# The last LayerNorm of a two-layer decoder: the mean taken from a column of weight sums, the squares of three quarters of the columns taken beside the last product, the square root on ScalarE

## Chip, cores and metric

The kernel runs on one core of one Trainium2 chip. The metric is device time in microseconds (us), as the median of several runs. Lower is better.

## The reference

What is computed is a decoder of two layers over 256 tokens of width 1024. Layer 0 mixes tokens with a gated spatial unit, layer 1 with causal attention; each is followed by a gated MLP with a short convolution. After each of the four sub-layers stands a residual sum and a LayerNorm. What matters here is the last one:

```python
def layer_norm(x, g, b):
    xf = x.astype(jnp.float32)
    mu = jnp.mean(xf, axis=-1, keepdims=True)
    var = jnp.mean(jnp.square(xf - mu), axis=-1, keepdims=True)
    y = (xf - mu) * lax.rsqrt(var + LN_EPS)
    return (y * g.astype(jnp.float32) + b.astype(jnp.float32)).astype(x.dtype)
...
    return (jax.nn.gelu(g) * val) @ w_down
...
        y = conv_ffn(x, f_w_up[i], f_conv_w[i], f_conv_b[i], f_w_down[i])
        x = layer_norm(DN_ALPHA * x + y, ln_ffn_g[i], ln_ffn_b[i])
```

`w_down` is 2816 x 1024. The result of the last `layer_norm` is the output, 256 x 1024 in float32.

## The kernel before, in words

All weights are streamed from memory in chunks of 128 x 2048 float32 into two buffers (`raw`). ScalarE rounds each half of a chunk to the matmul's reduced float32 format (`whi`), and VectorE takes the remainder (`wlo = raw - whi`); `prep` (L436) records both through `split` (L377). Five chunks are held at once, ten tiles of 1024 columns each in `whi` and in `wlo`. A product of full accuracy is then three matmuls: high by high, high by low, low by high (`rows_step`, L622).

Nothing is emitted in the order of the source. Each step is recorded as an operation with an engine, a price in ns and its dependences (`Plan.op`, L90). `Plan.emit` (L125) simulates the five engines with these prices: TensorE's main stream keeps the order of recording, and on the other engines the operation with the earliest due time among the ready ones goes next. The result is a fixed program for each engine; each engine works its list in order and waits on semaphores.

The output projections, the last of them (`f_dn1`) among them, go through `project_out` (L652). The 256 tokens are two row tiles, t = 0 and t = 1. The sum runs over 22 tiles of 128 weight rows (k). For k = 0 to 15 both row tiles are accumulated together in four PSUM banks of 512 columns. For the last six k (`TAIL`), t = 0 is finished first, then t = 1. For t = 1 the right bank is added into `x` early (`add(*mine.pop())`, L689), and the last six k of the right half go into two fresh half-banks of 256 columns (`ends`, L690). So the very end of TensorE's work is, in this order: 18 matmuls of 512 columns for columns 0 to 511, 18 of 256 columns for 512 to 767, and 18 of 256 columns for 768 to 1023 (`cuts[1]`, L661).

As each piece is done, `stats` (L556) adds it into `x` on VectorE (L360) and takes its partial mean and variance (`bn_stats`, L563); after the third piece it joins the three (`bn_aggr`, L566), adds epsilon (L568), and GpSimd raises the sum to the power -0.5 (L569). Then `scaled` (L573) works on VectorE: two steps of 512 columns, (x - mean) * gamma, which need no power, and then four of 256 columns, x * rstd + beta, which do. Behind each of these four a store to the output is issued from SyncE's queue (L374). The row of gamma and beta is the tile `lnrow`.

All of VectorE's steps of the form (a op s) op b are recorded on L360, plain sums, products and differences on L356, all of ScalarE's on L350, all main matmuls on L338, so that the tile names and shapes tell them apart. `tensor_tensor_reduce` (L952, in the softmax) shows in the trace as CUSTOM_DVE_ANT_0 with a short READ_ACCUMULATOR behind it.

Of the kernel before, what the change touches and what calls it, by code (L numbers as in the profile page):

```python
# [237 lines left out]
def trunk_kernel(ctx: ExitStack, tc: tile.TileContext, a: dict, out: bass.AP):  # L238
# [8 lines left out]
    def tiles(name, n, cols, dtype=F32):  # L247
        return [sb.tile([P, cols], dtype, name=f"{name}{i}") for i in range(n)]

    whi, wlo = Ring(tiles("whi", 2 * CHUNKS, SUB, F32R)), Ring(tiles("wlo", 2 * CHUNKS, SUB, F32R))  # L250
    raws = Ring(tiles("raw", RAWS, CH))

    xt = sb.tile([P, 2 * KT * S], F32R, name="xt")
# [11 lines left out]
    def place(which, at, cols):  # L265

        t = rr if which == "rr" else ff
        prev = [b for s, e, b in owners[which] if s < at + cols and at < e]
        b = Buf(t[:, at:at + cols], prev)
        owners[which] = [x for x in owners[which] if not (at <= x[0] and x[1] <= at + cols)] + [(at, at + cols, b)]  # L270
        return b
# [80 lines left out]
    def dve(ns, emit, r, w):  # L352
        return plan.op("dve", ns, emit, r, w)
# [23 lines left out]
    def split(hi, lo, src, psum=False, by="act"):  # L377

        (hb, hp, hv), (lb, lp, lv), (xb, xp, xv) = hi, lo, src
        if by == "dve":  # L380
            dve(70 + 0.52 * flat(xv), lambda: nc.vector.tensor_copy(hv, xv), [(xb, xp)], [(hb, hp)])  # L381
        else:
            act(hv, xv, AF.Copy, [(xb, xp)], [(hb, hp)], psum=psum)
        return tt(lv, xv, hv.bitcast(F32), ALU.subtract, [(xb, xp), (hb, hp)], [(lb, lp)])
# [49 lines left out]
        return [(raw, b, e, s * SUB) for s in range(2) for b, e in cuts]  # L434

    def prep(i):  # L436
        subs = []
        for raw, b, e, at in pieces_of(i):
            if b == 0:
                hi, lo = whi.new(), wlo.new()  # L440
                subs.append((hi, lo))
            parts = range(b // 256, e // 256)
            low = split((hi, parts, hi.ap[:, b:e]), (lo, parts, lo.ap[:, b:e]),
                        (raw, parts if 2 * i < KHEAD else range((at + b) // 256, (at + e) // 256),
                         raw.ap[:, at + b:at + e]), by="act" if loads.get("low") else "dve")
            loads.setdefault("low", low)
        chunks[i] = subs

    FINE = set()
    for n in ("f_up0", "f_up1"):  # L450
        FINE |= set(range(where[n, 0], where[n, 5]))

    def sub(name, c, s):
        return chunks[where[name, c]][s]
# [41 lines left out]
    def ln_rows(i):  # L496
        b = rowring.new()
        src = a["lnrow"]
        o = load(b.ap, bass.AP(tensor=src.tensor, offset=src.offset + i * 2 * D, ap=[[0, P], [1, 2 * D]]), [b])
        if i == 0:  # L500
            o.after = loads[5]
        return b, b.ap.rearrange("p (a d) -> p a d", a=2)
# [70 lines left out]
    def scaled(r, x, st, mean, rstd, rows, to=None):  # L573
# [6 lines left out]
        for o, n in [(o, S) for o in range(0, D, S)]:  # L580
# [3 lines left out]
            if to is not None:  # L584
                load(to[:, sl], x[:, sl], (), [(r, parts)])

    def ln_back(r, st, mean, rstd, rows, t, li, h, l, waits):

        step = KT // len(waits)
        lc = lncol.ap.rearrange("p (i a k) -> p i a k", i=3, a=2)  # L590
        x = r.ap
        for k0 in range(0, KT, step):
            sl, parts = slice(k0 * P, (k0 + step) * P), range(k0 // 2, (k0 + step) // 2)
            ts(x[:, sl], x[:, sl], mean, rstd, ALU.subtract, ALU.mult,
               [(r, parts), (st, ["mv", "rstd"])], [(r, parts)])

        def rest():
            rb, rv = rows
            for op, j in ((ALU.mult, 0), (ALU.add, 1)):
                for o in (0, HALF):  # L600
                    sl, parts = slice(o, o + HALF), range(o // S, (o + HALF) // S)
                    tt(x[:, sl], x[:, sl], rv[:, j, sl], op, [(r, parts), rb], [(r, parts)])

        def turn(k0):
            pt, x32 = bank(), (x32a if step == 4 else x32b).new()
            transposes([(pt.ap[:, j * P:(j + 1) * P], x[:, (k0 + j) * P:(k0 + j + 1) * P]) for j in range(step)],
                       [(r, range(k0 // 2, (k0 + step) // 2))], [pt])
            for j in range(step):
                k = k0 + j
                act(x32.ap[:, j * P:(j + 1) * P], pt.ap[:, j * P:(j + 1) * P], AF.Identity, [pt, lncol], [(x32, [j])],  # L610
                    bias=lc[:, li, 1, k:k + 1], scale=lc[:, li, 0, k:k + 1], psum=True)
            parts = [(t, k) for k in range(k0, k0 + step)]
            split((h, parts, xt_view(h)[:, t, k0:k0 + step, :]), (l, parts, xt_view(l)[:, t, k0:k0 + step, :]),
                  (x32, range(step), x32.ap.rearrange("p (k c) -> p k c", k=step)))
            if k0 + step == KT:
                plan.later(REST[li], rest)

        for wait, k0 in zip(waits, range(0, KT, step)):
            plan.later(wait, lambda k0=k0: turn(k0))


    def rows_step(pieces, hk, lk, r, hi, lo, first, last, into=None):  # L622


        groups = []
        for i, (o, n, b) in enumerate(pieces):
            parts = range(o // 256, (o + n) // 256)
            seq = [(b.ap[:, :n], x, w.ap[:, o:o + n], first and j == 0, last and j == 2)
                   for j, (x, w) in enumerate([(hk, hi), (hk, lo), (lk, hi)])]
            if into is not None:  # L630
                into += [(i, (0, 2, 1)[j], q) for j, q in enumerate(seq)]
            groups.append(mms(seq, r + [(hi, parts), (lo, parts)], [b], into=into,
                              ready=into is not None and len(into) == 12))
        plan.tick()
        return groups
# [16 lines left out]
    def project_out(name, nk, at, xold, li, rows_i):  # L652

        last = li is None

        rows = None if name == "b_o" else ln_rows(rows_i)


        free = [bank(True) for _ in range(2 * NT)]
        pieces = [[(o, HALF, free[2 * t + o // HALF]) for o in (0, HALF)] for t in range(NT)]  # L660
        cuts = [[(0, HALF), (HALF, HALF)], [(0, HALF), (HALF, S), (HALF + S, S)]]  # L661
        ends = []

        def step(t, k, which, first=0, last=nk - 1):
            hi, lo = sub(name, k // 2, k % 2)
            hk, lk, r = at(k, t)
            return rows_step(which, hk, lk, r, hi, lo, k == first, k == last)

        start = nk - TAIL
        early = [(k, t) for k in range(start) for t in range(NT)]  # L670
        for k, t in sorted(early, key=lambda x: x[1]) if nk == KT else early:
            step(t, k, pieces[t][:1])
            groups = step(t, k, pieces[t][1:], last=nk - 1 if t == 0 else start - 1)
            if name == "f_dn0" and (k, t) == (3, NT - 1):
                state["table"].after = groups[-1]
            if k % 2 and t == NT - 1:
                spent(name, k // 2)
        res = (None, None) if last else xt_new()
        for t in range(NT):
            r, x = xold[t], xold[t].ap  # L680

            def add(o, n, b, by=ALPHA):
                parts = range(o // S, (o + n) // S)
                stt(x[:, o:o + n], x[:, o:o + n], by, b.ap[:, :n], ALU.mult, ALU.add, [(r, parts), b], [(r, parts)])
                done_with(b)

            mine = list(pieces[t])
            if t == NT - 1:
                add(*mine.pop())  # L689
                ends = [(o, n, half()) for o, n in cuts[t][1:]]  # L690
                mine += ends
            both = start, nk - 2 if t == 0 and nk == KT else start
            turns = [(p, k) for k in range(*both) for p in mine] + [(p, k) for p in mine for k in range(both[1], nk)]
            for p, k in turns:
                if t == 0 and k == nk - 2:
                    plan.tick(AHEAD)
                step(t, k, [p], first=start if p in ends else 0)
            if t == NT - 1:
                for k in range(start, nk, 2):
                    spent(name, k // 2)  # L700

            rows = rows or ln_rows(rows_i)
            st, mean, rstd = stats(r, x, cuts[t], lambda j, o, n: add(*mine[j], 1.0 if mine[j] in ends else ALPHA))
            if last:
                scaled(r, x, st, mean, rstd, rows, out[t * P:(t + 1) * P, :])
            else:
                ln_back(r, st, mean, rstd, rows, t, li, *res, T0_WAITS if t == 0 else T1_WAITS)
        return res
# [428 lines left out]
```

## Time and profile before

| | |
|---|---|
| median of 3 runs | 563.37 us (563.23 to 564.23) |
| profiled execution, its own time | 563.43 us |
| profiled execution, span from first to last instruction | 561.7 us |
| granted TensorE clock, mean | 0.996 |
| busy: TensorE / VectorE / ScalarE / GpSimd | 98% / 83% / 64% / 2% |

The time of an execution is its span and 1.7 us around it. In the lists of groups, the first time is the group's busy total in us and the second the mean of one instruction in ns; in timelines and in the chain of waits the first number is the start in us from the span's start, the second the length in us. Several rows of one kind that follow each other are merged, with their count behind an x, and the brackets tell how long the engine sat idle ahead of a row and what ended that. PE is TensorE, DVE is VectorE, ACT is ScalarE, POOL is GpSimd, SPq is SyncE's queue of transfers.

### The profile page before, as it was taken

Reading aid. Unit: us, or ns where it says so; the run is one execution under the profiler, and the core shown is the slowest. Engines: PE = TensorE matmul, PEld = TensorE weight load, DVE = VectorE, ACT = ScalarE, POOL = GpSimd, SP = SyncE. Lnnn points to the kernel's source line nnn. Section 1 sums busy time; section 2 is a strip of 40 time slices with the busy share of each in tenths; the row PEclk is TensorE's granted clock in tenths of the full one; section 3 lists DMA queues with packets and bytes.
Section 4 is the critical chain, followed back from the end, with each engine's and each line's share of the span. In section 5 each row is a group of like instructions: output and inputs, shape, how many; then the busy total and the mean of one; then the engine's idle time right before and its main releaser. Section 6 shows DMA issues by size and latency. Waiting matters only on the chain.

```text
span 561.7 us, 8289 instructions
## 1 busy us (share of the span) xinstructions
PE 552.4 (98%) x3042; PEld 473.7 (84%) x3042; DVE 467.8 (83%) x902; ACT 361.3 (64%) x679; POOL 11.2 (2%) x18
## 2 busy tenths in 40 slices
PE   9999999999999999999999999999999999999994
PEld 6888788988988888888888888788888988888884
DVE  5798989999899989558868778899999999998326
ACT  6647577777777667425677867587777787685200
POOL 0020000000000000001000000000000000000001
PEclk9999999999999999999999999999999999999998
DMA  8987445756645366852657252725667454557202
GB/s 320 371 307 280 160 149 175 276 175 219 235 196 183 117 242 219 301 192 79 232 207 220 87 182 82 293 88 195 245 228 285 162 221 156 200 202 272 75 1 75
DMA packets 19569, 110.97 MB, mean 198 GB/s; under 512 B 2295, under 2 KB 5577, under 8 KB 7369
## 3 DMA queue, kind: packets, MB, share of 16 engines
q1 hardware_dynamic: 19528, 110.44, 54.8%
q8 instruction: 24, 0.39, 0.3%
q14 instruction: 17, 0.13, 0.1%
HBM read 109.36 MB, written 1.07 MB: 197 GB/s over the span
## 4 chain that ended last, share of the span: by engine, by line
PE 92%; DMA 3%; DVE 3%; ACT 1%; issue 0%; DVEq 0%; ACTq 0%
PE bank L338 58%; PE twos L338 32%; DMA raw<-in_a_out 1%; PE twos L344 1%; DMA raw<-in_a_u 1%; PE bank L344 1%; DVE wlo L356 1%; DVE ff L356 1%; DMA ff<-in_head 1%; DVE x L360 0%; ACT whi L350 0%; DVE rr L356 0%; ACT rr L350 0%; DVE stat L563 0%; DVE whi L381 0%
## 5 line engine op out<-in xcount | busy, mean ns | idle before, releaser
L356 DVE TENSOR_TENSOR wlo<-raw,whi 128x1024 fp32r<-128x1024 f32 (+1 forms) x202 | 220.2, 1114 | 28.4 <-ACT whi L350 28.1
L350 ACT ACTIVATE whi<-raw 128x1024 fp32r<-128x1024 f32 (+1 forms) x202 | 187.5, 966 | 41.6 <-DMA raw<-in_f_dn 16.8
L338 PE MATMUL bank<-whi,rr 128*128 128x512 f32 x432 | 135.7, 391 | 0.5 <-DVE ff L356 0.5
L338 PE MATMUL bank<-xt,whi 128*128 128x512 f32 x512 | 121.2, 391 | 0.0
L338 PEld LDWEIGHTS bank<-xt,whi 128*128 128x128 f32 x512 | 94.7, 188 | 18.7
L338 PEld LDWEIGHTS bank<-whi,rr 128*128 128x128 f32 x432 | 81.1, 188 | 18.1 <-DVE ff L356 0.9
L338 PE MATMUL bank<-wlo,rr 128*128 128x512 f32 x216 | 84.1, 389 | 0.0
L338 PE MATMUL twos<-xt,whi 128*128 128x512 f32 x320 | 74.4, 390 | 0.0
L360 DVE SCALAR_TENSOR_TENSOR ff<-ff,convc 128x255 f32<-128x255 f32 (+1 forms) x160 | 69.5, 478 | 3.1 <-ACT ff L350 2.6
L338 PEld LDWEIGHTS twos<-xt,whi 128*128 128x128 f32 x320 | 59.4, 188 | 11.9
L338 PEld LDWEIGHTS bank<-xt,wlo 128*128 128x128 f32 x512 | 64.2, 191 | 2.0 <-issue 0.3
L338 PE MATMUL bank<-xt,wlo 128*128 128x256 f32 x512 | 65.6, 284 | 0.0
L350 ACT ACTIVATE ff<-ff,convc 128x256 f32<-128x256 f32 x80 | 45.1, 593 | 10.4 <-DVE ff L356 10.3
L338 PEld LDWEIGHTS bank<-wlo,rr 128*128 128x128 f32 x216 | 40.6, 188 | 8.1
L338 PE MATMUL twos<-whi,xt 128*128 128x512 f32 x128 | 42.1, 396 | 0.0
L350 ACT ACTIVATE ff<-ff 128x256 f32<-128x256 f32 x52 | 20.5, 412 | 31.8 <-DVE rr L356 26.0
L338 PEld LDWEIGHTS twos<-xt,wlo 128*128 128x128 f32 x320 | 39.7, 192 | 0.8
L338 PE MATMUL twos<-xt,wlo 128*128 128x256 f32 x320 | 40.0, 283 | 0.0
L350 ACT ACTIVATE ff<-bank 128x256 f32<-128x256 f32 (+2 forms) x62 | 24.2, 394 | 16.0 <-PE bank L338 14.7
L350 ACT ACTIVATE ff<-bank,lncol 128x128 f32<-128x128 f32 x48 | 18.9, 459 | 22.8 <-PE bank L344 18.8
L338 PEld LDWEIGHTS twos<-whi,xt 128*128 128x128 f32 x128 | 24.1, 188 | 4.7
L350 ACT ACTIVATE ff<-twos 128x512 f32<-128x512 f32 (+1 forms) x34 | 17.7, 551 | 15.7 <-PE twos L338 13.0
(88 smaller groups left out, 514.2 us busy)
## 6 DMA issues: line engine op xcount, KB each, us to landing
raw<-in_f_up SPq DMA_DIRECT2D x44, 1024.0 KB, 4.8
raw<-in_f_dn SPq DMA_DIRECT2D x22, 1024.0 KB, 4.8
raw<-in_b_qk SPq DMA_DIRECT2D x8, 1024.0 KB, 4.8
lnrow<-in_lnrow SPq DMA_DIRECT2D x5, 1024.0 KB, 8.4
raw<-in_a_out SPq DMA_DIRECT2D x4, 1024.0 KB, 7.0
raw<-in_b_v SPq DMA_DIRECT2D x4, 1024.0 KB, 4.8
raw<-in_b_o SPq DMA_DIRECT2D x4, 1024.0 KB, 4.8
raw<-in_a_u SPq DMA_DIRECT2D x3, 1024.0 KB, 9.4
```

The costliest lines, as they stand in the source:

```text
L338: nc.tensor.matmul(o, l, x, start=start, stop=stop)
L344: nc.tensor.transpose(o, x, ident.ap)
L350: return plan.op("act", ns, lambda: nc.scalar.activation(o, x, func, **kw), r, w, table=table)
L356: return dve(70 + 1.04 * flat(x), lambda: nc.vector.tensor_tensor(o, x, y, op=op), r, w)
L360: lambda: nc.vector.scalar_tensor_tensor(o, x, s, y, op0=op0, op1=op1), r, w)
```

## The change

Only the last normalization, and of it only t = 1, gets a new form; it needs a sum of weights that is made ahead.

- `whi` and `wlo` tiles get two more columns. For the three chunks of the last six k of `f_dn1` (`SUMMED`), VectorE sums the weights of columns 512 to 767 of each row, splits the sum into high and low part, and puts it into the two columns (twice the same).
- The last two pieces of t = 1 change places, and the last but one takes the sums along: 18 matmuls of 258 columns give columns 768 to 1023 and the row sum of the product that is still to come (columns 512 to 767).
- `close` replaces `stats` and `scaled` for t = 1. The early-added part of columns 512 to 767 is put through `bn_stats` at once, columns 0 to 511 when they are done; the piece of 256 columns is added by a `tensor_tensor_reduce` that also gives its sum and starts from the sum of the coming product. So the mean of all 1024 columns is known before the last product is.
- Under the last product: ScalarE takes the squares of 768 columns with an accumulated sum; VectorE subtracts the mean from columns 512 to 767 in place and makes (x - mean) * gamma for the other 768. Gamma has been scaled by the square root of 1024 on ScalarE beforehand, into a part of `ff`.
- Behind the last product: VectorE adds it; GpSimd multiplies these 256 columns by gamma; VectorE takes their squares' sum; ScalarE takes the square root of the total; VectorE inverts it and makes three steps y * rstd + beta, of 512, 256 and 256 columns, each with its store.

```diff
-    whi, wlo = Ring(tiles("whi", 2 * CHUNKS, SUB, F32R)), Ring(tiles("wlo", 2 * CHUNKS, SUB, F32R))
+    whi, wlo = (Ring(tiles(n, 2 * CHUNKS, SUB + 2, F32R)) for n in ("whi", "wlo"))
...
+            if i in SUMMED and e == SUB:
+                if sums is None:
+                    sums = stat.new()
+                    both_subs = raw.ap[:, :CH].rearrange("p (a c) -> p a c", a=2)[:, :, HALF:HALF + S]
+                    dve(70 + 1.04 * 2 * S, lambda: nc.vector.tensor_reduce(
+                        sums.ap[:, :2], both_subs, axis=mybir.AxisListType.X, op=ALU.add),
+                        [(raw, [2, 6])], [sums])
+                split((hi, [4], hi.ap[:, SUB:]), (lo, [4], lo.ap[:, SUB:]),
+                      (sums, [0], sums.ap[:, at // SUB:at // SUB + 1].to_broadcast([P, 2])), by="dve")
...
+    SUMMED = set(range(where["f_dn1", (FT - TAIL) // 2], where["f_dn1", FT // 2 - 1] + 1))
...
+    def close(r, x, own, rows, to):
...
+        act(gd.ap, rv[:, 0], AF.Copy, [rb], [gd], scale=D ** 0.5)
...
+        def summed(o, v, w, op, first, to, r, w_):
+            dve(70 + 1.04 * flat(v), lambda: nc.vector.tensor_tensor_reduce(
+                out=o, in0=v, in1=w, scale=1.0, scalar=first, op0=op, op1=ALU.add, accum_out=to), r, w_)
+
+        some(1, x2, p2)
+        act(junk.ap[:, :1], st.ap[:, 6:7], AF.Sqrt, [(st, [("st", 1)])], [junk], table="sqrt")
+        stt(x0, x0, ALPHA, b0.ap[:, :n0], ALU.mult, ALU.add, [(r, p0), b0], [(r, p0)])
+        some(0, x0, p0)
+        dve(90, lambda: nc.vector.bn_aggr(st.ap[:, 12:14], st.ap[:, :12]), [(st, [("st", 0), ("st", 1)])], [(st, ["mv"])])
+        dve(70, lambda: nc.vector.tensor_scalar_mul(known, mean, (n0 + n2) / D), [(st, ["mv"])], [(st, ["known"])])
+        summed(x1, x1, b1.ap[:, :n1], ALU.add, b1.ap[:, n1:n1 + 1], total, [(r, p1), b1], [(r, p1), (st, ["total"])])
+        dve(130, lambda: nc.vector.scalar_tensor_tensor(less, total, -1.0 / D, known, op0=ALU.mult, op1=ALU.subtract),
+            [(st, ["total", "known"])], [(st, ["less"])])
+        less_ = (st, ["less"])
+        for j, v, p, to_ in ((j0, x0, p0, ss0), (j1, x1, p1, ss1)):
+            act(j, v, AF.Square, [(r, p), less_], [(junk, [p[0]]), (st, [("ss", j is j1)])], bias=less, accum=to_)
+        act(rest, ss1, AF.Identity, [(st, [("ss", False), ("ss", True)])], [(st, ["rest"])], bias=ss0)
+        dve(190, lambda: nc.vector.tensor_scalar(x2, x2, less, None, op0=ALU.add), [(r, p2), less_], [(r, p2)])
+        for v, w, g, p in ((y0, x0, g0, p0), (y1, x1, g1, p1)):
+            stt(v, w, less, g, ALU.add, ALU.mult, [(r, p), less_, gd], [(y, p)])
+        tt(x2, x2, b2.ap[:, :n2], ALU.add, [(r, p2), b2], [(r, p2)])
+        plan.op("pool", 1060, lambda: nc.gpsimd.tensor_tensor(y2, x2, g2, op=ALU.mult), [(r, p2), gd], [(y, p2)])
+        summed(j2, x2, x2, ALU.mult, D * EPS, ssl, [(r, p2)], [(junk, [p2[0]]), (st, ["ssl"])])
+        act(rstd, ssl, AF.Sqrt, [(st, ["ssl", "rest"])], [(st, ["std"])], bias=rest, table="sqrt")
+        dve(80, lambda: nc.vector.reciprocal(rstd, rstd), [(st, ["std"])], [(st, ["rstd"])])
+        for o, v, p in ((o0, y0, p0), (o1, y1, p1), (o2, y2, p2)):
+            stt(v, v, rstd, rv[:, 1, o:o + flat(v)], ALU.mult, ALU.add, [(y, p), (st, ["rstd"]), rb], [(y, p)])
+            load(to[:, o:o + flat(v)], v, (), [(y, p)])
...
-        cuts = [[(0, HALF), (HALF, HALF)], [(0, HALF), (HALF, S), (HALF + S, S)]]
+        cuts = [[(0, HALF), (HALF, HALF)], [(0, HALF), (HALF + S, S + 2), (HALF, S)] if last else
+                [(0, HALF), (HALF, S), (HALF + S, S)]]
...
+            if last and t == NT - 1:
+                close(r, x, mine, rows, out[t * P:(t + 1) * P, :])
+                break
```

What the emitted programs hold at three places. First VectorE's list before, from the sum of columns 0 to 511 of t = 1 (`bank_106`) to its end; `twos_104` and `twos_105` are the two pieces of 256 columns, `stat_91` the statistics of t = 1, `stat_90` those of t = 0.

```order
L360 SCALAR_TENSOR_TENSOR x<-x,bank_106 128x512
L360 SCALAR_TENSOR_TENSOR x<-x,stat_90,lnrow_89 128x256
L563 BN_STATS stat_91<-x 128x6
L360 SCALAR_TENSOR_TENSOR x<-x,twos_104 128x256
L563 BN_STATS stat_91<-x 128x6
L360 SCALAR_TENSOR_TENSOR x<-x,twos_105 128x256
L563 BN_STATS stat_91<-x 128x6
L566 BN_AGGR stat_91<-stat_91 128x2
L568 TENSOR_SCALAR stat_91<-stat_91 128x1
L360 SCALAR_TENSOR_TENSOR x<-x,stat_91,lnrow_89 128x512 x2
L360 SCALAR_TENSOR_TENSOR x<-x,stat_91,lnrow_89 128x256 x4
```

And VectorE's list now, from the sum of the last piece but one (L616 is the `tensor_tensor_reduce` of `close`, with the readout of its accumulator as the second ISA row) to the end; `stat_90` now holds the statistics of t = 1, and `ff` holds gamma and y.

```order
L616 ISA x,stat_90<-x,twos_104 128x256
L616 ISA stat_90 128x1
L623 BN_AGGR stat_90<-stat_90 128x2
L624 TENSOR_SCALAR stat_90<-stat_90 128x1
L626 SCALAR_TENSOR_TENSOR stat_90<-stat_90 128x1
L632 TENSOR_SCALAR x<-x,stat_90 128x256
L360 SCALAR_TENSOR_TENSOR ff<-x,stat_90,ff 128x512
L360 SCALAR_TENSOR_TENSOR ff<-x,stat_90,ff 128x256
L356 TENSOR_TENSOR x<-x,twos_105 128x256
L616 ISA ff,stat_90<-x 128x256
L616 ISA stat_90 128x1
L639 RECIPROCAL stat_90<-stat_90 128x1
```

Between the two pieces of 256 columns there were two instructions; now eight stand between the sums of `twos_104` and `twos_105`. Behind the sum of `twos_105` there were nine instructions; now there are six: the three shown and the three y * rstd + beta (one of 512 columns, two of 256).

The end of ScalarE's list, as a difference; `lnrow_89` holds gamma, the `whi` rows are the last three weight chunks. It had no work behind these before, and now has the table load, a first square root of one column, the squares, the sum of the two square sums and the square root that counts.

```order
+L350 ACTIVATE ff<-lnrow_89 128x1024
+L350 ACTIVATE whi_67<-raw_85 128x1024
+L350 ACTIVATE whi_68<-raw_85 128x1024
+L350 ACTIVATE whi_69<-raw_86 128x1024
+L350 ACTIVATE whi_70<-raw_86 128x1024
+L350 ACTIVATE whi_71<-raw_85 128x1024
+L350 ACTIVATE whi_72<-raw_85 128x1024
+L350 ACT_TABLE_LOAD
+L350 ACTIVATE ff<-stat_90 128x1
+L350 ACTIVATE ff,stat_90<-x,stat_90 128x512
+L350 ACTIVATE ff,stat_90<-x,stat_90 128x256
+L350 ACTIVATE stat_90<-stat_90 128x1 x2
```

The scaling of gamma now stands ahead of the split of the last three chunks, and there is one table load, ahead of the first square root, and none behind it.

The sums of weights go into VectorE's list ahead of the remainders of the last three chunks; this is the first of the three (`raw_85` the loaded chunk, `whi_67` to `wlo_78` its tiles, of which the 128x2 rows fill the new columns).

```order
L451 TENSOR_REDUCE stat_90<-raw_85 128x2
L381 CAST whi_67<-stat_90 128x2
L381 CAST whi_68<-stat_90 128x2
L356 TENSOR_TENSOR wlo_77<-stat_90,whi_67 128x2
L356 TENSOR_TENSOR wlo_78<-stat_90,whi_68 128x2
L356 TENSOR_TENSOR wlo_77<-raw_85,whi_67 128x1024
L356 TENSOR_TENSOR wlo_78<-raw_85,whi_68 128x1024
```

Before, only the last two of these rows stood there. SyncE's list keeps its loads in order and ends with stores of 512, 256 and 256 columns in the place of four of 256.

More of the change, by code (lines that the diff above doesn't have):

```diff
@@ L436, in prep @@
     def prep(i):
-        subs = []
+        subs, sums = [], None
         for raw, b, e, at in pieces_of(i):
@@ L585, in scaled, with some @@
                 load(to[:, sl], x[:, sl], (), [(r, parts)])
+    def close(r, x, own, rows, to):
+        rb, rv = rows
+        (o0, n0, b0), (o1, n1, b1), (o2, n2, b2) = own
+        n1 -= 2
+        st = stat.new()
+        s = st.ap[:, :12].rearrange("p (a b) -> p a b", b=6)
+        mean, known, total, less, ss0, ss1, rest, ssl, rstd = (st.ap[:, i:i + 1] for i in (12, *range(14, 22)))
+        y, gd, junk = (place("ff", i * D, D) for i in range(3))
+        part = lambda o, n: range(o // S, (o + n) // S)
+        p0, p1, p2 = part(o0, n0), part(o1, n1), part(o2, n2)
+        (x0, x1, x2), (y0, y1, y2), (g0, g1, g2), (j0, j1, j2) = ([t[:, o:o + n] for o, n, _ in ((o0, n0, 0), (o1, n1, 0), (o2, n2, 0))]
+                                                                  for t in (x, y.ap, gd.ap, junk.ap))
+        act(gd.ap, rv[:, 0], AF.Copy, [rb], [gd], scale=D ** 0.5)
+        def some(j, v, p):
+            dve(70 + 1.04 * flat(v), lambda: nc.vector.bn_stats(s[:, j, :], v), [(r, p)], [(st, [("st", j)])])
+        def summed(o, v, w, op, first, to, r, w_):
[25 more added lines that the diff above has]
+            load(to[:, o:o + flat(v)], v, (), [(y, p)])
@@ L626, in rows_step @@
         for i, (o, n, b) in enumerate(pieces):
-            parts = range(o // 256, (o + n) // 256)
+            parts = range(o // 256, -(-(o + n) // 256))
             seq = [(b.ap[:, :n], x, w.ap[:, o:o + n], first and j == 0, last and j == 2)
```

## The prediction

> **What bounds the kernel.** I read the page first, then the chain of waits of the last 40 us, then the timelines of its engines. TensorE is busy for 552.4 us of the 561.7, and the chain of the end shows where the other 9 lie: the first row here is from the page, the second from the view of cores, the rest from the chain.
>
> ```profile
> PE 552.4 (98%) x3042; PEld 473.7 (84%) x3042; DVE 467.8 (83%) x902; ACT 361.3 (64%) x679; POOL 11.2 (2%) x18
> core 0: 561.7 us, clock 0.996
> ...
> 549.84 4.32 PE twos L338 x36
> ...
> 554.18 0.43 DVE x L360
> ...
> 554.64 0.44 DVE stat L563
> ...
> 555.10 0.25 DVE stat L566
> ...
> 555.37 0.15 DVE stat L568
> 555.53 0.72 DVE x L360 x2
> 556.25 0.52 issue
> 556.77 0.48 DVE x L360
> 557.24 0.40 DVEq L1133
> 557.64 0.79 DVE x L360 x2
> ```
>
> TensorE runs without a gap up to 554.16; everything behind it is a tail in series on VectorE. The 0.52 of "issue" is a wait for GpSimd's power, as the first row of the next timeline shows (555.67 + 0.92 = 556.59); the two others are the last stores.
>
> ```profile
> 555.67 0.92 POOL L569 TENSOR_TENSOR stat<-stat,nhalf 128x1 f32<-128x1 f32 x1 [6.96 <-DVE stat L568]
> ...
> 558.18 0.40 SPq L374 DMA_DIRECT2D out<-x  x1
> ...
> 558.67 0.39 SPq L374 DMA_DIRECT2D out<-x  x1
> ```
>
> The last step of VectorE ends at 557.64 + 0.79 = 558.43. The queue issues stores 0.49 apart here, so the last goes out at 558.67, 0.24 behind its data. From there to the end are 561.70 - 558.67 = 3.03 us, which I keep. So the change can win only what it takes from 554.18 to 558.67, 4.49 us.
>
> **What lies ahead of the tail.** Three sums of weights with four small splits each on VectorE, and 1024 columns of gamma on ScalarE, are new.
>
> ```profile
> 516.17 2.01 ACT L350 ACTIVATE whi<-raw 128x1024 fp32r<-128x1024 f32 x2 [2.92 <-DMA raw<-in_f_dn]
> ...
> 527.85 1.23 DVE L356 TENSOR_TENSOR wlo<-raw,whi 128x1024 fp32r<-128x1024 f32 x1 [1.12 <-ACT whi L350]
> 537.63 0.69 DVE L360 SCALAR_TENSOR_TENSOR x<-x,bank 128x512 f32<-128x512 f32 x1 [8.56 <-PE bank L338]
> ```
>
> ScalarE waits 2.92 us for a load where gamma goes, and one such instruction is about 1 us (two in 2.01). VectorE is through with the weights at 529.08 and then idle for 8.56 us. What queues behind the sums are only the remainders of the same chunks, which wait for the same loads. Bounds: nothing, or, without this cover, some 1 us on ScalarE and 3 on VectorE. I take nothing. The 18 wider matmuls stream 258 columns for 256: 36 lie within 4.32 us, 0.12 each, so 18 x 0.12 x 2/256 = 0.02 us.
>
> **The new tail, step by step.** Lengths, from the groups by shape:
>
> ```profile
> L360 DVE SCALAR_TENSOR_TENSOR x<-x,stat,lnrow 128x256 f32<-128x256 f32 x8 | 3.4, 478 | 0.0
> L360 DVE SCALAR_TENSOR_TENSOR x<-x,stat,lnrow 128x512 f32<-128x512 f32 x4 | 2.8, 744 | 0.0
> L952 DVE CUSTOM_DVE_ANT_0 ff<-twos,ff 128x256 f32<-128x256 f32 x16 | 6.0, 419 | 1.2 <-PE twos L338 1.2
> L961 DVE TENSOR_SCALAR ff<-ff,smax 128x256 f32<-128x256 f32 x16 | 5.1, 343 | 0.0
> L959 DVE RECIPROCAL smax<-smax 128x2 f32<-128x2 f32 x16 | 2.6, 162 | 2.2 <-ACT ff L350 2.1
> L350 ACT ACTIVATE ff<-ff,smax 128x256 f32<-128x256 f32 x16 | 8.0, 501 | 1.1 <-DVE smax L955 1.1
> L350 ACT ACTIVATE ff<-ff,smax 128x128 f32<-128x128 f32 x16 | 6.2, 390 | 0.0
> L350 ACT ACTIVATION_READ_ACCUMULATOR ff<-ff,smax 128x1 f32 x32 | 6.1, 190 | 0.0
> L350 ACT ACTIVATE ff<-ff,convc 128x256 f32<-128x256 f32 x80 | 45.1, 593 | 10.4 <-DVE ff L356 10.3
> L350 ACT ACTIVATE ff<-ff 128x256 f32<-128x256 f32 x52 | 20.5, 412 | 31.8 <-DVE rr L356 26.0
> L1051 ACT ACTIVATE spare<-spare 128x1 f32<-128x1 f32 x1 | 0.2, 203 | 0.0
> L350 ACT ACT_TABLE_LOAD x2 | 2.6, 1283 | 0.0
> L360 DVE SCALAR_TENSOR_TENSOR ff<-ff,convc 128x255 f32<-128x255 f32 x80 | 37.4, 479 | 3.1 <-ACT ff L350 2.6
> ```
>
> And the spacing: instructions of VectorE that wait for nothing overlap by some 0.08 (two of 744 ns in 1.40, two of 478 in 0.87), while dependent ones follow 0.03 behind the end before (554.61 to 554.64 above).
>
> ```profile
> 552.03 0.42 DVE L360 SCALAR_TENSOR_TENSOR x<-x,twos 128x256 f32<-128x256 f32 x1 [0.28 <-PE twos L338]
> ...
> 555.44 1.40 DVE L360 SCALAR_TENSOR_TENSOR x<-x,stat,lnrow 128x512 f32<-128x512 f32 x2
> ...
> 557.56 0.87 DVE L360 SCALAR_TENSOR_TENSOR x<-x,stat,lnrow 128x256 f32<-128x256 f32 x2
> ```
>
> *Under the last product.* The sum with accumulation starts at 552.05; its start value is read through a pointer, so I take 0.48, the 256-column row with a pointer, not 0.42. Then, each 0.03 behind the other: joining the statistics 0.24 (552.80), scaling 0.15 (552.98), the mean's negative 0.15 (553.16), the subtraction over 256 columns 0.34 (553.53). The two products with gamma overlap: started at 553.46 and 554.12, so VectorE is free at 554.52. What queues behind its first wait, for TensorE at 552.05, is also the joining of the statistics, which could have run before it: some 0.45 us of this chain stand there by the order alone. The last product has been ready since 554.16. **Its sum so starts 0.34 later than now (554.18) and ends at 554.94.** That is the price of preparing under the last product. ScalarE's squares start at 553.2: 0.39 for 128 and 0.50 for 256 columns give 0.72 for 512, then 0.50, readout 0.19 and one small step 0.3: done by 554.9, ahead of need.
>
> *Behind it.* Squares' sum 0.42 (555.39, its readout within the overlap); square root 555.43: 0.20 for one column and 0.09 for each pointer that is read (two pointers make 593 of 412 ns), 0.29, to 555.72; inverse 0.16 (555.91). Then y * rstd + beta: 555.94 to 556.68, the next 0.66 and 0.40 apart, ending at 557.08 and 557.48. Stores at 556.71, 557.20 and 557.69; the first is now the larger one, and if the last queues behind its data, that costs at most one step of the queue, 0.49, of which I take nothing, since it is issued 0.98 behind it. Against 558.67 **a gain of 0.98 us, if GpSimd disturbs nothing.**
>
> *GpSimd.* Its 256-column product is released with the sum of squares, at 554.94, and no row shows one. What rows show is whom it waits for:
>
> ```profile
> 254.46 0.55 POOL L569 TENSOR_TENSOR stat<-stat,nhalf 128x1 f32<-128x1 f32 x1 [175.32 <-DVE stat L568]
> ...
> 264.05 1.22 DVE L356 TENSOR_TENSOR wlo<-raw,whi 128x1024 fp32r<-128x1024 f32 x1
> 264.28 1.40 POOL L569 TENSOR_TENSOR stat<-stat,nhalf 128x1 f32<-128x1 f32 x1 [9.27 <-DVE stat L568]
> ...
> 28.76 1.09 POOL L508 TENSOR_SCALAR_AFFINE_SELECT ff<-ff 128x1024 f32<-128x1024 f32 x1 [27.36 <-DMA ff<-in_wsT]
> ...
> 29.55 0.85 DVE L360 SCALAR_TENSOR_TENSOR ff<-ff,stat,lnrow 128x512 f32<-128x512 f32 x1
> ...
> masks.py:199 POOL TENSOR_SCALAR_AFFINE_SELECT ident<-ident 128x128 f32<-128x128 f32 x1 | 0.3, 295 | 0.1
> ```
>
> The same one-column power takes 0.55 with VectorE idle and 1.40 beside a two-input step of VectorE: it ends 0.41 behind that step (265.68 against 265.27). So GpSimd's product starts in earnest behind the sum of squares, at 555.39. Its length: 0.41 at least; (1094 - 295)/896 = 0.89 ns per column of one input, doubled for two, is 0.45 for 256, so 0.86, to 556.25. The other way round, the step at 29.55 took 0.85 for 0.74 although GpSimd's operation ran 0.30 us into it: the hold ended 0.19 before GpSimd's recorded end. So y * rstd may be held from 555.94 to 556.06, 0.12 us. **Sum: 0.98 - 0.12 = 0.86, I say 0.9 us.** Bounds of this term: 0, and all of GpSimd's time, below.
>
> The Trainium skill, "SBUF — State Buffer", section "Who interferes with whom", says that a VectorE instruction with two inputs in SBUF and a GpSimd instruction that reads SBUF exclude each other, and that the later one blocks fully until the first is through. The 0.55 and 1.40 agree; the 0.85 shows less than a full block. The "GPSIMD Engine Reference", section "Engine selection", would leave elementwise work to VectorE; its 4497 ns for 2048 columns would make, as an estimate, 0.56 for 256, and the gain 0.1 smaller.
>
> **Rivals.**
>
> *Above the forecast, under 562.24.* If the small steps are shorter than their rows, or the two products with gamma start sooner, so that the last sum starts at 554.2 as now, 0.34 come back: 0.98 + 0.34 = 1.3, at 562.1. For it: ScalarE and the mean's chain have slack. Against: eight instructions in 2.1 us of PE time add up to 2.5 by their rows. Chance 0.32 with all between.
>
> *A full hold.* GpSimd holds VectorE to its end, and two inputs cost more than twice one: 0.41 + 0.75 after 555.39 is 556.55; y starts 0.6 later, the gain is 0.4: 563.0. For it: the 1.40. Chance 0.16. This is the rule of "SBUF — State Buffer" in the Trainium skill to the letter.
>
> *The root not prepared.* Were a second table load between squares and root, it would cost 1.28 (the row of table loads) and bring 563.4 - 0.9 + 1.28 = 563.8; for it speaks that square and square root are two functions, against it that the order shows one load only, ahead of both. Chance 0.04.
>
> *Slower: the row pitch.* Every `whi` and `wlo` row grows from 4096 to 4104 bytes, so most tiles start off their old boundaries, and 3042 matmuls (first row above) read them nearly all. If a shifted row costs TensorE time, it costs it throughout: 1 ns each is 3.0 us and 563.4 - 0.9 + 3.0 = 565.5; from 0.3 ns on it eats the 0.9, from 0.7 on the kernel is slower by over 0.2%. Against: VectorE reads rows shifted by one element at no price (the 479 of the 255-column steps against the 478 of 256 columns). Nothing shows TensorE doing so. Chance 0.06, with a product of GpSimd that lasts over 4 us instead of 0.9.
>
> **How the numbers follow.** 0.2% is 1.13 us, about what a measurement can tell from no change. The forecast (chance 0.42) is 563.43 - 0.9 = 562.53, and the median stands 0.06 below the profiled run: 562.5, within 0.2%. Faster: 0.32. Same: 0.42 + 0.16 + 0.04 = 0.62. Slower: 0.06. Range: 561.8 (everything in the first rival and 0.3 of spread) to 563.3 (the full hold and the same spread); outside are the pitch, the table and the rim of the first rival, under 0.2.
>
> **What would show it.** Right: the last matmul ends where it did, the last sum starts 0.2 to 0.4 us behind it, GpSimd's product ends about 0.4 plus half a us behind the sum of squares, the first y * rstd of 512 columns is longer than 0.74 or late by 0.1, and the last store is issued near 557.8. Wrong: TensorE's last matmul elsewhere than 554.2 by over half a us; the last sum at 554.2; a wait of VectorE for GpSimd ahead of the last step; a table load behind the squares.

## The result, and the profile after

The changed kernel takes 570.49 us (median of 6 runs, 568.97 to 571.58) beside 563.3 us for the kernel before (6 runs, 562.78 to 565.06): a ratio of 1.0113, 95% interval 1.0094 to 1.0131. It is slower by 7.2 us where 562.5 was forecast. The profiled execution is the longest of the six, 571.58 us.

The page and the view of cores, after:

```profile
PE 559.9 (98%) x3042; PEld 472.5 (83%) x3042; DVE 472.1 (83%) x921; ACT 365.5 (64%) x688; POOL 11.3 (2%) x18
core 0: 569.9 us, clock 0.997
```

TensorE has as many matmuls as before, at the same clock, and is busy 7.5 us longer (559.9 against 552.4). The tail behind it is the new one. VectorE, from the accumulating sum on (L616, which was L360 in the kernel before), then the last matmul, GpSimd and the square root:

```profile
560.26 0.49 DVE L616 CUSTOM_DVE_ANT_0 x<-x,twos 128x256 f32<-128x256 f32 x1 [0.39 <-PE twos L338]
...
562.62 0.41 DVE L356 TENSOR_TENSOR x<-x,twos 128x256 f32<-128x256 f32 x1
563.06 0.43 DVE L616 CUSTOM_DVE_ANT_0 ff<-x 128x256 f32<-128x256 f32 x1
...
563.92 0.16 DVE L639 RECIPROCAL stat<-stat 128x1 f32<-128x1 f32 x1 [0.42 <-ACT stat L350]
564.12 1.54 DVE L360 SCALAR_TENSOR_TENSOR ff<-ff,stat,lnrow 128x512 f32<-128x512 f32 x3
```

```profile
562.06 0.28 PE L338 MATMUL twos<-whi,rr 128*128 128x256 f32 x1
```

```profile
563.16 0.91 POOL L636 TENSOR_TENSOR ff<-x,ff 128x256 f32<-128x256 f32 x1 [6.33 <-DVE x L356]
```

```profile
563.60 0.30 ACT L350 ACTIVATE stat<-stat 128x1 f32<-128x1 f32 x1 [0.61 <-DVE stat L616]
```

The place to measure from is the start of the step on the last piece but one. It stood at 552.03 before and stands at 560.26 now, 8.23 later. From there to VectorE's last end it was 558.43 - 552.03 = 6.40 and is 564.12 + 1.54 - 560.26 = 5.40: the tail is 1.0 shorter. What comes after is 1.0 longer: the stores of the output, after, and the last line of the same view, before.

```profile
L374 SPq DMA_DIRECT2D out<-ff x3: 332/402/412, 564.9 to 565.8; - x3
...
DMA to landing us min/median/max: 1.9/2.0/3.0
```

```profile
DMA to landing us min/median/max: 1.9/2.0/2.0
```

From the issue of the last store to the span's end it is 569.9 - 565.8 = 4.1 in the place of 3.0. So the spans differ by 8.2 - 1.0 + 1.0 = 8.2. Two things need a cause: 7.5 us of TensorE, and 1 us of the last store. The other 0.7 of the 8.23 is idle time of TensorE at 57 to 59 us, where the group of the first row below begins: it waited 1.2 us for VectorE in this execution and 0.5 before.

**TensorE.** Its groups by shape, first after, then before: the streamed operand stands first behind the arrow, the stationary one second.

```profile
L338 PE MATMUL bank<-whi,rr 128*128 128x512 f32 x432 | 138.0, 396 | 1.2 <-DVE ff L356 1.2
L338 PE MATMUL bank<-xt,whi 128*128 128x512 f32 x512 | 123.4, 395 | 0.0
L338 PE MATMUL bank<-wlo,rr 128*128 128x512 f32 x216 | 85.1, 394 | 0.0
...
L338 PE MATMUL bank<-xt,wlo 128*128 128x256 f32 x512 | 64.6, 281 | 0.0
...
L344 PE MATMUL twos<-ident,ff 128*128 128x128 f32 x58 | 7.8, 272 | 0.0
```

```profile
L338 PE MATMUL bank<-whi,rr 128*128 128x512 f32 x432 | 135.7, 391 | 0.5 <-DVE ff L356 0.5
L338 PE MATMUL bank<-xt,whi 128*128 128x512 f32 x512 | 121.2, 391 | 0.0
L338 PE MATMUL bank<-wlo,rr 128*128 128x512 f32 x216 | 84.1, 389 | 0.0
...
L338 PE MATMUL bank<-xt,wlo 128*128 128x256 f32 x512 | 65.6, 284 | 0.0
...
L344 PE MATMUL twos<-ident,ff 128*128 128x128 f32 x58 | 7.8, 272 | 0.0
```

Every product with the weights at 512 columns takes 4 or 5 ns more, whether the weights are streamed or stationary. Those of 256 columns take 3 less, and those without weights the same. The single records agree: from one start to the next the median goes from 227 to 232 ns at 512 columns and from 120 to 118 at 256. Before, most intervals are exactly 226 or 227; after, they scatter from 224 to 238. The loss is spread over the kernel: 1.2 us by matmul 100 (0.8 of it in the first 20), 3.6 by 1000 (0.7 of it that idle time), 5.8 by 2000 and 8.2 by 3000. So it isn't the end of the kernel that got slower but all of it. The prediction's own rival of the row pitch is the place to look.

**The last store.** Transfers in the last microseconds, after, by queue:

```profile
q1 hardware_dynamic: 432, 0.52, 24.2%
q14 instruction: 1, 0.01, 0.3%
```

And before:

```profile
q1 hardware_dynamic: 576, 0.52, 26.2%
```

The second row after is a fetch of instructions, one packet of 8 KB. It begins at 567.4 and takes 0.3. Only nine packets of the stores start behind it, eight of 1 KB and one of 4 bytes. They come one behind the other, the last at 568.3, while ahead of the fetch many overlap. That is how it would look if they shared one of the 16 transfer engines with the fetch; the trace doesn't name the engine of a packet. Before, the last fetch of this kind was at 476.3, and the stores were alone at the end.

### The profile page after: what moved, and what is told of

Its sections match the earlier page's. It is cut to its first block, busy times and chain, and to the rows that moved or that the text cites. A ratio compares the mean times of both kernels' runs of the same rounds, so it can differ in the third digit from the quotient of the medians.

```text
span 569.9 us, 8314 instructions
## 1 busy us (share of the span) xinstructions
PE 559.9 (98%) x3042; PEld 472.5 (83%) x3042; DVE 472.1 (83%) x921; ACT 365.5 (64%) x688; POOL 11.3 (2%) x18
## 4 chain that ended last, share of the span: by engine, by line
PE 92%; DMA 4%; DVE 2%; ACT 1%; issue 1%; DVEq 0%; ACTq 0%
PE bank L338 58%; PE twos L338 32%; DMA raw<-in_a_out 2%; PE twos L344 1%; PE bank L344 1%; DMA raw<-in_a_u 1%; DVE wlo L356 1%; ACT whi L350 1%; DMA ff<-in_head 1%; DVE ff L356 0%; DVE ff L360 0%; ACT uparts L350 0%; ACT ff L350 0%; DVE x L616 0%; DVE whi L381 0%
## 5 line engine op out<-in xcount | busy, mean ns | idle before, releaser
L338 PE MATMUL bank<-whi,rr 128*128 128x512 f32 x432 | 138.0, 396 | 1.2 <-DVE ff L356 1.2
L338 PE MATMUL bank<-xt,whi 128*128 128x512 f32 x512 | 123.4, 395 | 0.0
L338 PE MATMUL twos<-xt,whi 128*128 128x512 f32 x320 | 76.0, 394 | 0.0
L360 DVE SCALAR_TENSOR_TENSOR ff<-ff,convc 128x255 f32<-128x255 f32 (+1 forms) x160 | 69.3, 477 | 3.6 <-ACT ff L350 3.1
L360 DVE SCALAR_TENSOR_TENSOR x<-x,bank 128x512 f32<-128x512 f32 x16 | 10.9, 684 | 21.9 <-PE bank L338 21.9
```

Of the source, the lines that this page charges most:

```text
L338: nc.tensor.matmul(o, l, x, start=start, stop=stop)
L360: lambda: nc.vector.scalar_tensor_tensor(o, x, s, y, op0=op0, op1=op1), r, w)
```

## Experiments

**What was to be told apart.** For TensorE: (1) the place of streamed and stationary operand relative to each other within 256 bytes. Before, `whi`, `wlo`, `xt` and `rr` all begin 128 bytes behind a multiple of 256. After, the weight tiles, padded to 4128 bytes, begin at 128, 160, 192, 224, 0 and so on, and `xt` and `rr` behind them at 0. (2) The new pitch by itself. (3) The place of an operand against a fixed boundary. (4) The new work: the sums of weights, or what they do to ScalarE and VectorE. For the store: the instruction fetch, or the wider store of 512 columns.

**Pitch only.** The kernel before with the wider tiles, of which nothing else is used.

```diff
-    whi, wlo = Ring(tiles("whi", 2 * CHUNKS, SUB, F32R)), Ring(tiles("wlo", 2 * CHUNKS, SUB, F32R))
+    whi, wlo = (Ring([t[:, :SUB] for t in tiles(n, 2 * CHUNKS, SUB + 2, F32R)]) for n in ("whi", "wlo"))
```

> The kernel before, with the rows of the weight tiles 4104 bytes long in the place of 4096 (laid out 4128 apart), the two new columns unused; no other step changes. Theory A (the place of the weight rows in memory slows TensorE's streaming): 568 to 572 us, 512-column matmuls 4 to 5 ns longer (395 for 391) throughout. Theory B (the new work costs it: sums on VectorE, gamma on ScalarE, 258 columns, the new tail): 563 to 564.

Measured: 569.88 us (569.45 to 570.1, 4 runs) against 563.59, ratio 1.0103 [1.0083, 1.0123]. Its groups:

```profile
L338 PE MATMUL bank<-whi,rr 128*128 128x512 f32 x432 | 137.8, 396 | 0.3 <-DVE ff L356 0.3
L338 PE MATMUL bank<-xt,whi 128*128 128x512 f32 x512 | 123.4, 395 | 0.0
```

These are the matmul times of the changed kernel. Two unused columns a tile cost 6.3 of the 7.2 us, which the two intervals don't tell apart, and bring TensorE's busy time to 559.4 us, of 559.9 in the changed kernel. The new work costs TensorE nothing that shows.

**The change with a pitch of a multiple of 256 bytes.** The whole change, with 64 columns more in a tile in the place of 2, so that the weight tiles, `xt` and `rr` are all back at 128.

```diff
-    whi, wlo = (Ring(tiles(n, 2 * CHUNKS, SUB + 2, F32R)) for n in ("whi", "wlo"))
+    whi, wlo = (Ring(tiles(n, 2 * CHUNKS, SUB + 64, F32R)) for n in ("whi", "wlo"))
...
-                split((hi, [4], hi.ap[:, SUB:]), (lo, [4], lo.ap[:, SUB:]),
+                split((hi, [4], hi.ap[:, SUB:SUB + 2]), (lo, [4], lo.ap[:, SUB:SUB + 2]),
```

> The changed kernel with all its steps, but the weight rows 4352 bytes apart (4096 + 256), so that all tiles begin at the same offset within 256 bytes again, as in the kernel before. Theory A: the matmuls are back at 391 and the last product ends near 554.2; the time is 562.2 to 563.5, by whether the tail keeps its 1.0 us on VectorE or loses it to the instruction fetch seen behind the last store. Theory B: 569 to 571.5 as in the changed kernel.

Measured: 562.87 us (562.25 to 564.26, 10 runs), ratio 0.9991 [0.9978, 1.0004]. Its groups, and its stores:

```profile
L338 PE MATMUL bank<-whi,rr 128*128 128x512 f32 x432 | 135.4, 391 | 0.0
L338 PE MATMUL bank<-xt,whi 128*128 128x512 f32 x512 | 121.2, 391 | 0.0
...
L338 PE MATMUL bank<-xt,wlo 128*128 128x256 f32 x512 | 65.6, 284 | 0.0
```

```profile
DMA to landing us min/median/max: 1.9/2.0/3.0
```

TensorE is back at its old pace though the pitch is larger still, 4352 bytes: this pitch by itself costs nothing. The late fetch is still there (at 558.7), and with it the 3.0 us of the last store: the tail's gain of 1.0 is given back, and no difference can be measured.

**A gap of 128 bytes behind the weights, and 32 bytes ahead of everything.** Both are the kernel before and one unused tile. In the first the weights stay at 128, and all tiles allocated behind them move by 128 bytes, `xt` and `rr` to 0; in the second all move together, from 128 to 160.

```diff
+    sb.tile([P, 32], F32, name="gap")
     raws = Ring(tiles("raw", RAWS, CH))
```

> The kernel before with an unused tile of 128 bytes between the weight tiles and all tiles behind them: the weight rows stay where they were and 4096 apart, while the activations (xt, rr) move by 128 bytes. Theory A1 (what counts is where streamed and stationary rows lie to each other, within 256 bytes): slower, 567 to 572. Theory A2 (what counts is the weight rows' own pitch or boundary): 563 to 564. Theory B: 563 to 564.

```diff
+    sb.tile([P, 8], F32, name="gap")
     whi, wlo = Ring(tiles("whi", 2 * CHUNKS, SUB, F32R)), Ring(tiles("wlo", 2 * CHUNKS, SUB, F32R))
```

> The kernel before with an unused tile of 32 bytes ahead of all: every tile moves by 32 bytes, all still alike within 256. Theory A1 (only relative place counts): 563 to 564. Theory A3 (rows must start on a 64- or 128-byte boundary): slower, 567 to 572. Theory B: 563 to 564.

Measured: the first 571.17 us (570.76 to 572.82, 4 runs), ratio 1.0136 [1.0107, 1.0164]; the second 563.35 us (562.8 to 564.34, 10 runs), ratio 0.9991 [0.998, 1.0002]. The groups of the first, then of the second:

```profile
L339 PE MATMUL bank<-whi,rr 128*128 128x512 f32 x432 | 137.7, 396 | 0.0
L339 PE MATMUL bank<-xt,whi 128*128 128x512 f32 x512 | 123.9, 396 | 0.0
```

```profile
L339 PE MATMUL bank<-whi,rr 128*128 128x512 f32 x432 | 135.3, 391 | 0.0
L339 PE MATMUL bank<-xt,whi 128*128 128x512 f32 x512 | 121.2, 391 | 0.0
```

With no row's length or pitch changed, 128 bytes between the operands make the whole slowdown. 32 bytes under all of them make none, so a fixed boundary of 64 bytes or more isn't it. What counts is how streamed and stationary operands lie to each other.

**A gap of 128 bytes ahead of `rr` alone.** Then only products with `rr` as the stationary operand have their operands apart; those with `xt` and the weights keep theirs.

```diff
+    sb.tile([P, 32], F32, name="gap")
```

> The kernel before with an unused tile of 128 bytes ahead of rr, the activations that the output projections use: weights and xt stay as they were, only rr (and ff behind it) moves by 128 bytes against the weights. Theory A1 (a matmul is slower where the streamed and the stationary operand begin at different offsets within 256 bytes): matmuls between rr and the weights 395 to 396 in the place of 391, those between xt and the weights still 391; about 760 of 512 columns by 5 ns are 3.8 us, less 1 for those of 256: 566 to 567.5. Rival (any move of the tiles against the weights, or DMA and split on the raw tiles, slows all): 570 to 572, all matmuls 395; or none: 563 to 564.

Measured: 566.65 us (566.46 to 567.34, 4 runs), ratio 1.0059 [1.0046, 1.0071]. Its groups:

```profile
L339 PE MATMUL bank<-whi,rr 128*128 128x512 f32 x432 | 137.9, 396 | 0.0
L339 PE MATMUL bank<-xt,whi 128*128 128x512 f32 x512 | 121.3, 391 | 0.0
L339 PE MATMUL bank<-wlo,rr 128*128 128x512 f32 x216 | 85.2, 394 | 0.0
```

The products with `rr` are slow, those with `xt` are not. (432 + 216) x 5 ns = 3.2 us, which is what TensorE is busy more in this profile (555.6 against 552.4).

**The sums of weights split on ScalarE.** The kernel with the pitch of a multiple of 256 bytes, where the small splits are two steps of ScalarE each. VectorE carries out 12 instructions fewer, which puts the end of its list ahead of the point where the late fetch begins. The three stores are as before it.

```diff
-                split((hi, [4], hi.ap[:, SUB:SUB + 2]), (lo, [4], lo.ap[:, SUB:SUB + 2]),
-                      (sums, [0], sums.ap[:, at // SUB:at // SUB + 1].to_broadcast([P, 2])), by="dve")
+                one, h2, l2 = sums.ap[:, at // SUB:at // SUB + 1], hi.ap[:, SUB:SUB + 2], lo.ap[:, SUB:SUB + 2]
+                act(h2, one.to_broadcast([P, 2]), AF.Copy, [(sums, [0])], [(hi, [4])])
+                act(l2, h2.bitcast(F32), AF.Identity, [(sums, [0]), (hi, [4])], [(lo, [4])], bias=one, scale=-1.0)
```

> The changed kernel with weight rows 4352 bytes apart, as in the second run, and with the split of the weight sums moved from VectorE to ScalarE: 12 instructions fewer on VectorE, 12 more on ScalarE, in their idle time. Theory C (the 16 instructions that the change adds to VectorE bring a fetch of 8 KB of instructions just behind its last step, and on one transfer engine the last store waits for it): no such fetch behind the last store, the last store lands within 2.0 to 2.2 us of its issue in the place of 3.0, and the time is 561.6 to 562.3. Rival (the store of 512 columns ahead of the last two delays them): still 3.0 us, and 562.5 to 563.2.

Measured: 562.22 us (561.72 to 563.54, 12 runs) against 563.46, ratio 0.9979 [0.997, 0.9987]. All transfers of the last 5 us by queue, and the stores:

```profile
DMA packets 432, 0.52 MB, mean 105 GB/s; under 512 B 48, under 2 KB 304, under 8 KB 432
## 3 DMA queue, kind: packets, MB, share of 16 engines
q1 hardware_dynamic: 432, 0.52, 29.9%
```

```profile
DMA to landing us min/median/max: 1.9/2.0/2.2
```

Only the stores are left, and the slowest lands in 2.2 us, the 512-column store among them. So the wider store isn't the cause. With the fetch gone the change wins 1.2 us, about the 1.0 that its tail wins.

**Sixteen idle instructions.** The kernel before, with 16 memsets of one column on VectorE, which nothing reads, at about 538 us, where it was idle anyway.

```diff
+                if last:
+                    for _ in range(16):
+                        dve(70, lambda: nc.vector.memset(idle, 0.0), [(r, range(2, 4))], [spare_])
```

> The kernel before with 16 memsets of one column on VectorE, in its idle time at 538 us, so that its list is as long as in the changed kernel. Theory C: one more instruction fetch near the end of the span, behind VectorE's last step, and 0.3 to 1.1 us more, if it meets the last store's data: 563.7 to 564.6. Rival (16 instructions in idle time cost nothing): no change, 563.0 to 563.6.

Measured: 564.1 us (563.72 to 565.25, 11 runs), ratio 1.0015 [1.0006, 1.0024]: 0.85 us more by the ratio, 0.64 by the medians (563.46 before). Its last transfers and its stores:

```profile
q1 hardware_dynamic: 576, 0.52, 26.6%
q14 instruction: 1, 0.01, 0.8%
```

```profile
DMA to landing us min/median/max: 1.9/2.0/3.0
```

The late fetch can be called up in the kernel before by the number of VectorE's instructions alone, and it lengthens the last landing as in the changed kernel. In the traces such a fetch comes about every 128 instructions that VectorE carries out (waits counted). In the three kernels where VectorE has 1090, the last one comes at the 1087th; the kernel before has 1074 and the version with the sums on ScalarE 1078, and neither has it.

**The mean's chain put ahead.** The kernel with the sums on ScalarE and two added dependences, so that the joining of the statistics and the scaling come ahead of the accumulating sum, and both products with gamma ahead of the last sum.

```diff
-        summed(x1, x1, b1.ap[:, :n1], ALU.add, b1.ap[:, n1:n1 + 1], total, [(r, p1), b1], [(r, p1), (st, ["total"])])
+        summed(x1, x1, b1.ap[:, :n1], ALU.add, b1.ap[:, n1:n1 + 1], total, [(r, p1), b1, (st, ["known"])], [(r, p1), (st, ["total"])])
...
-        tt(x2, x2, b2.ap[:, :n2], ALU.add, [(r, p2), b2], [(r, p2)])
+        tt(x2, x2, b2.ap[:, :n2], ALU.add, [(r, p2), b2, (y, p1)], [(r, p2)])
```

> The kernel with the pitch of 256 bytes and the sums split on ScalarE, with the joining of the statistics and the scaling of the known mean put ahead of the accumulating sum, and both products with gamma ahead of the last sum. By the step of the prediction that put the price of preparing under the last product at 0.34 us, by the order alone: the accumulating sum starts some 0.15 us later (about 2.6 us ahead of the last sum now 2.36), but the last sum then starts at the end of the last matmul, 0.2 us earlier against the last matmul than in the kernel it is made from, and everything behind it moves with it: 0.2 us less, 562.0 us against 562.2, too little for the times to tell and to be read in the trace (start of the last sum minus end of TensorE about 0.03 to 0.05 instead of 0.24). Rival: the chain from the accumulating sum to the last sum is set by the length of its instructions whatever their order (they add up to what TensorE takes), the last sum keeps its distance of 0.2 us, and the time is the same. Neither expects TensorE's matmuls (391, 389, 284 ns) or the landing of the last store (2.0 to 2.2 us) to change.

Measured: 562.17 us (561.66 to 562.68, 7 runs) against 563.3, ratio 0.9975 [0.9964, 0.9987]. Its last matmul, and VectorE:

```profile
554.09 0.28 PE L338 MATMUL twos<-whi,rr 128*128 128x256 f32 x1
```

```profile
552.25 0.15 DVE L625 TENSOR_SCALAR stat<-stat 128x1 f32<-128x1 f32 x1
552.32 0.48 DVE L617 CUSTOM_DVE_ANT_0 x<-x,twos 128x256 f32<-128x256 f32 x1
...
554.41 0.42 DVE L356 TENSOR_TENSOR x<-x,twos 128x256 f32<-128x256 f32 x1
```

The last sum starts 0.04 behind the last matmul (554.41 - 554.37). In the changed kernel it is 0.28 (562.62 - 562.34), so the wait there was one of order. The times of this and the version before it can't be told apart, as expected; both are faster than the kernel before and than the changed one.

## Why the prediction was wrong

**The step that failed is the one that left TensorE alone.** The forecast charged it 0.02 us for 18 wider matmuls. The row pitch was seen, but as a rival at 0.06, with 1 ns per matmul, 3.0 us and 565.5. It was held down by "VectorE reads rows shifted by one element at no price". That row speaks of another engine and of a shift of one operand alone. The runs showed 4 to 5 ns more at 512 columns and 3 less at 256: TensorE was busy 7.5 us longer over 3042 matmuls, 2.5 ns on average. The rival's place and its sign were right. Its price was too small, and its mechanism, a row off a boundary, was not it: rows 32 bytes off run at full pace if the other operand is off by the same. With nothing in the trace of before to price it, the range should have reached over it, as every matmul with weights stood behind it.

**"3.03 us, which I keep" failed too.** The end behind the last store grew by 1.0 us, because the change gave VectorE enough more instructions to reach a fetch at the wrong time. That is all that the tail won, so without the pitch there would have been no change that can be told (0.9991) in the place of the forecast 0.9 of gain. The Trainium skill, "Runtime: NRT & Kernel Launch", section "Instruction fetch mechanics", has each engine's instruction memory refilled in blocks of 16 KiB, 256 instructions, and calls its cost mostly hidden. In this trace VectorE's block is 8 KB, for about 128 instructions (the measurement decides). No wait of an engine for it shows at the end, but the store's last packets come behind it.

**The tail was sized right.** Counted from the step on the last piece but one (predicted from 552.05, measured from 560.26):

| step | predicted | measured |
|---|---|---|
| last sum starts | 2.47 | 2.36 |
| squares' sum starts | 2.92 | 2.80 |
| square root starts | 3.38 | 3.34 |
| inverse starts | 3.70 | 3.66 |
| last y step ends | 5.43 | 5.40 |

The 0.34 that preparing under the last product was to cost came out as 0.26 (0.28 behind the matmul where it was 0.02 before), and the version with the chain put ahead won it back in the trace (0.04 behind the matmul); the times can't tell it. The eight instructions on which that rested were right in kind and 0.1 us too long in sum. That the sums of weights and gamma are hidden was right too: with the pitch mended TensorE is busy 552.7 us, against 552.4.

**GpSimd's hold was not there.** 0.12 us were charged for it. The product was recorded at 0.91, against 0.86 from 555.39 on. It begins here 0.10 behind VectorE's sum of squares, and ends at 564.07, ahead of the y step at 564.12, which takes its full pace (three steps in 1.54, as sized). If it was held behind the sum of squares to 563.49, 0.58 is left for its work; that was not tried.

**The other rivals.** One table load stayed one. The full hold did not come. The first rival's cause, a tail shorter than its rows, holds for the 0.1 us in the table's first rows only.

**What stays open.** Why the relative place of the operands matters isn't known. The stationary operand of the next matmul is loaded while the current one streams (after, the load of 57.44 to 57.63 us lies within the matmul of 57.33 to 57.83), so two reads that meet are a guess, which no run tests by itself. Offsets of 32 to 224 bytes were seen only mixed, in the changed kernel. There, the single records show that a product's own two operands are not all that counts (share of intervals at the old 226 or 227 ns, 512 columns):

- `xt` streamed, against the one tile of `whi` at `xt`'s own place: all 50 with two such products ahead and one behind. The ten at the end of such a run, whose next product has weights that lie elsewhere, all took 235 ns.
- `xt` streamed, against each of the other nine tiles of `whi`: 0 to 22%.
- That one tile streamed, against `xt` or `rr` at its own place, by turns with its low part, which lies 64 bytes off: 5% of 64.

So the neighbours' operands count too, which fits the guess and doesn't prove it. The 0.7 us that TensorE idled more at 57 to 59 us in the profiled execution wasn't pursued. The version with the pitch only shows none of it (0.3 us there), and the profiled execution is 1.1 us over the median.

## What to carry to other kernels

A tile's width is a layout for all tiles behind it. If the matmuls' streamed and stationary operands lay alike within 256 bytes, pad by a multiple of 256 bytes, and look at the matmuls' mean by shape in every profile after a change of tiles. When a change touches what every instruction of the bound engine reads, put its unknown price times their number into the range, and don't argue it away by a row of another engine. At the very end look past the last instruction too: a dozen more or fewer instructions on one engine can put a fetch ahead of the last store.

## What the runs showed of the hardware

- A matmul of 512 columns in reduced float32 is issued every 227 ns where its operands and its neighbours' lie alike within 256 bytes, and every 232 where they are 128 bytes apart or mixed (medians); at 256 columns it is 120 and 118 to 119. Multiples of 256 between them cost nothing (tiles 4352 bytes apart: 391 ns, as before). For the kernel it is 6.3 to 7.6 us of 563.
- The Trainium skill, "SBUF — State Buffer", section "Who interferes with whom", says that TensorE never waits on anyone. No run tests whether another engine can hold its reads. Its pace does hang on where its own operands lie: 396 against 391 ns with nothing changed but an unused tile.
- An instruction fetch of 8 KB that begins while the last store is under way made it land in 3.0 us in the place of 2.0 to 2.2, in all three kernels that had one there.
